# Reordering the step table of an SSD layer: conv product, z weight, skip product, output scale and weight slices

## The chip, the cores and the metric

The kernel runs on one core of one Trainium2 chip. The metric is device time in microseconds (us), from the start to the end of one execution; three executions are timed and the median stands. The engines are TensorE (PE in the profile, with its weight loads as PEld), VectorE (DVE), ScalarE (ACT), GpSimd (POOL) and SyncE (SP), which here issues nearly all transfers.

## The reference

The reference is one inference step of a two-layer decoder over 1024 prompt rows and 8 x 8 sample rows of width 1024, in float32: a Mamba-2 SSD layer, then a latent attention (MLA) layer, then a norm. Only the SSD layer is touched.

```
proj = h @ w_in                           # -> z (2048), x | B | C (2048 + 1024 + 1024), dt (32 heads)
xbc  = silu(causal_conv(xbc, w[0..3]) + b)
dt   = softplus(dt_raw + dt_bias);  a = cumsum(dt * a_head)       # per head, in chunks of 128 rows
M    = exp(a_l - a_s) * (l >= s)
y    = (C B^T * M) (x dt) + (C . state) * exp(a)                  # state runs from chunk to chunk
y    = (y + d_skip * x) * silu(z)
y    = y * rsqrt(mean over a group of 256 (y^2) + eps) * norm_w   # 8 groups
out  = y @ w_out                                                  # 2048 -> 1024
```

B and C are shared by the four heads (256 columns) of a group; there are 8 groups. The outputs are the layer's rows, the final state for the prompt and for each sample, and the last three rows before the convolution.

## The kernel before, in words

Float32 matmuls are done as three products of two-part numbers: a `split` makes a high part (an ACT cast, `L130`, e.g. `wih` from the raw weight `wraw`) and a low part (a subtraction on DVE or POOL, `L131`, e.g. `wil`), and PE multiplies high by high, low by high and high by low.

The layer goes through the 8 groups in a pipeline. While group g-1 is scanned (`Scan`), group g is projected and convolved (`Flow`). `ssd_groups` is one table of steps, written out by hand: from here on the order in which an engine gets its instructions is exactly the order of the calls (the part ahead of it in `layer_ssd` is ordered by a planner). Seven iterations have 21 steps each (t = 0 to 20). A step calls, in this order: `fl.proj(t)` (projection on PE; t = 0 to 11 are the four conv blocks B, C, x, x of 128 channels in three column pieces, t = 12 to 20 are z for nine row tiles), the next weight part's split and load, `scan.ew(t)` (elementwise work of the scan), `fl.ew(t)` (elementwise work of the convolution), `ev()` (ACT copies the projection from PSUM into `raw` or `z`), `fl.after(t)`, `scan.pe(t)` and `fl.pe(t)` (matmuls of the scan, transposes).

In `Scan`, chunk i (0 to 7 for the prompt, 8 for the samples) has its even step t = 2i and its odd step t = 2i+1. The odd step calls `front1(i+1)`: the decay matrix M, for which the cumulative sums are loaded from memory (`M<-acs_d`), ACT relus (`L717`), the Exp (`L723`), the casts of C (`Ch`) and of the weighted x (`xddh`). The `skip` product `xD = x * d_skip` is on POOL (`L731`), `out2` adds it (`L779`), multiplies by the gate (`L786`) and squares with a sum (`L787`) into `yssq`. The samples' states come three at a time: `copies` (`xr`, POOL `L795`), transposes `x3p`, block products `sn`, and the split of the old state `s0p` into `sh` and `sl` for the product `pv`. `split(11)` is the last part of z's weight; it comes at t = 11 behind all of `scan.ew`.

The convolution of a block in `fl.ew` is an ACT product with the fourth tap (`L617`, `acc<-raw`), then three DVE multiply-adds (`L621`) in steps t = 3(b+1) to 3(b+1)+2 for block b, over 128 x 1112 elements.

Behind the groups stands the output stage, a loop of 45 steps. The last group is scanned in its first 22. The product with `w_out` goes in two halves: `OutProj` a over slices 0 to 7 (groups 0 to 3) from step A0 = 7, and b over slices 8 to 15 from step B0 = 25, each over nine row tiles, two steps a tile. A tile of y is loaded back from memory (`yta`, `ytb`), scaled by the reciprocal root of its group's mean square (`scale`, one POOL multiplication, `L998`), transposed on PE (`ytpa`, `ytpb`, `L1008`), split, and multiplied (`poa`, `pob`). `WOut` loads slices of 512 KB (`wraw`) and splits them with the norm weight folded in (`woh` on ACT, `L1062`; `wol` on DVE, `L1068`). `group_rstd` computes the reciprocal roots with a POOL power (`L1087`).

At the start, `layer_ssd` projects group 0, then `ssd_dt` computes dt and the cumulative sums and stores them to memory, and `ssd_groups` begins with the first chunk's `load_decay`, `front`, `front1`, and then loads and splits group 1's first weight parts.

## Time and profile before

| what | value |
|---|---|
| three runs | 2110.97, 2112.72, 2114.36 us; median 2112.72 |
| profiled execution | 2108.55 us, its span 2106.5 us, granted clock 0.963 |
| PE busy | 1935.1 us (92% of the span) |
| DVE, ACT, POOL busy | 1251.3, 1078.6, 840.4 us |
| start of group 1 to the end of group 7 | about 126 to 863 us, 101.5 us for a middle group |
| output stage with the last scan | about 863 to 1032 us |
| output product alone | about 1032 to 1140 us, then the MLA layer |

The profile comes from one execution. A row of the timeline has the start, the duration, the engine, the line, the operation, the tile written and the tiles read with their shapes, and in brackets how long the engine was idle before it and what ended that wait. A row of the busy time by stretch has the stretch, its length, then for PE, PEld, DVE, ACT and POOL the busy time and the count, then the granted TensorE clock as a share of the full one, the share of the DMA engines that was busy, and GB/s. A row of the costliest groups has line, engine, operation, tiles and count, then busy time and mean ns, then the idle time before them.

### The profile page before, as it was taken

To read this page: it belongs to the slowest core of one execution; us is meant where nothing else is said; L and a number is where in the kernel's file an instruction comes from. 1 tells how busy PE (TensorE), PEld (TensorE's weight loads), DVE (VectorE), ACT (ScalarE), POOL (GpSimd) and SP (SyncE) were. 2 spreads that over 40 slices of the span, in tenths; PEclk is the share of its full clock that TensorE was granted. 3 is DMA by queue.
4 is the path that set the end of the run, shared out by engine and by line. 5 is a ranking of instruction groups with operands and counts; after the bars stand their busy time and mean duration, and the time that the engine had idled before them with its cause. 6 is when DMAs were issued, how large, how long until landed. Compare 5 with 4: busy or idle time off the path is not lost.

```text
span 2106.5 us, 33533 instructions
## 1 busy us (share of the span) xinstructions
PE 1935.1 (92%) x12001; PEld 1765.0 (84%) x12001; DVE 1251.3 (59%) x2540; ACT 1078.6 (51%) x2555; POOL 840.4 (40%) x1003
## 2 busy tenths in 40 slices
PE   6969999999999999589999999799999999889998
PEld 5969999999999998578787999698888788778887
DVE  4427575858585757534424305366787878776665
ACT  5345656565656565622203314244676667755552
POOL 0316464737474757433210001102333333765541
PEclk9979999999999999689999999899999999999999
DMA  4013232332323232533645333132111211464441
GB/s 144 20 54 88 82 86 82 90 88 80 91 85 92 81 88 75 169 115 131 199 152 183 112 139 86 41 108 78 47 42 43 63 38 54 131 194 137 143 148 43
DMA packets 186477, 206.54 MB, mean 98 GB/s; under 512 B 23132, under 2 KB 151912, under 8 KB 185928
## 3 DMA queue, kind: packets, MB, share of 16 engines
q1 hardware_dynamic: 181480, 185.40, 29.2%
q0 software_dynamic: 4752, 18.88, 2.8%
q8 instruction: 95, 1.56, 0.3%
q14 instruction: 70, 0.57, 0.1%
q10 hardware_dynamic: 80, 0.13, 0.0%
HBM read 151.05 MB, written 53.28 MB: 97 GB/s over the span
## 4 chain that ended last, share of the span: by engine, by line
PE 60%; DVE 15%; ACT 7%; issue 6%; DMA 6%; POOL 5%; SPq 1%; POOLq 0%; DVEq 0%; ACTq 0%
PE pj L89 19%; PE pq L101 5%; PE pob L101 4%; PE poa L101 4%; PE pj L101 3%; PE py L742 2%; POOL kvl L1961 2%; PE pk L101 1%; PE pz L101 1%; PE p L101 1%; DVE tl L1680 1%; PE vp L89 1%; DMA M<-acs_d 1%; PE st L1666 1%; PE st L1668 1%
## 5 line engine op out<-in xcount | busy, mean ns | idle before, releaser
L89 PE MATMUL pj<-xh,wih 128*128 128x384 f32 (+1 forms) x768 | 254.9, 336 | 18.4 <-ACT wih L130 9.8
L89 PE MATMUL pj<-xl,wih 128*128 128x384 f32 (+1 forms) x768 | 254.4, 331 | 0.0
L89 PE MATMUL pj<-xh,wil 128*128 128x384 f32 (+1 forms) x768 | 252.6, 329 | 0.0
L621 DVE SCALAR_TENSOR_TENSOR acc<-raw,vec,acc 128x1112 f32<-128x1112 f32 x84 | 138.0, 1643 | 77.7 <-ACT acc L617 77.7
L89 PEld LDWEIGHTS pj<-xh,wih 128*128 128x128 f32 x768 | 145.4, 190 | 20.1 <-ACT wih L130 10.1
L1680 POOL TENSOR_TENSOR tl<-P,th 128x384 fp32r<-128x384 f32 (+1 forms) x96 | 90.4, 942 | 179.1 <-ACT P L1678 143.5
L101 PE MATMUL pj<-wih,xh 128*128 128x256 f32 x504 | 144.2, 290 | 3.9 <-ACT wih L130 3.9
L89 PEld LDWEIGHTS pj<-xl,wih 128*128 128x128 f32 x768 | 146.2, 190 | 0.6
L89 PEld LDWEIGHTS pj<-xh,wil 128*128 128x128 f32 x768 | 145.8, 190 | 0.2 <-DVE wil L131 0.2
L101 PE MATMUL pj<-wil,xh 128*128 128x256 f32 (+1 forms) x504 | 140.0, 284 | 4.0 <-DVE wil L131 4.0
L1677 ACT ACTIVATE th<-st 128x512 fp32r<-128x512 f32 x192 | 94.1, 490 | 72.2 <-PE st L1673 53.3
L101 PE MATMUL pj<-wih,xl 128*128 128x256 f32 x448 | 126.7, 283 | 0.0
L131 DVE TENSOR_TENSOR wil<-wraw,wih 128x512 fp32r<-128x512 f32 x88 | 70.3, 802 | 92.0 <-ACT wih L130 91.6
L131 POOL TENSOR_TENSOR xddl<-xdd,xddh 128x256 fp32r<-128x256 f32 x64 | 65.5, 1024 | 127.5 <-ACT xddh L130 126.5
L779 POOL TENSOR_TENSOR y<-y,xD 128x256 f32<-128x256 f32 x64 | 77.9, 1217 | 78.0 <-DVE y L778 78.0
L1961 POOL TENSOR_TENSOR kvl<-pgr,kvh 128x1024 fp32r<-128x1024 f32 x32 | 78.2, 2444 | 65.6 <-ACT kvh L1960 65.6
L101 PEld LDWEIGHTS pj<-wih,xh 128*128 128x128 f32 x504 | 96.2, 191 | 5.3 <-ACT wih L130 5.3
L101 PEld LDWEIGHTS pj<-wil,xh 128*128 128x128 f32 (+1 forms) x504 | 93.2, 185 | 6.0 <-DVE wil L131 5.4
L717 ACT ACTIVATE M<-M,tok 128x128 f32<-128x128 f32 (+1 forms) x288 | 90.5, 388 | 11.5 <-DMA M<-acs_d 11.5
L1678 ACT ACTIVATE P<-st 128x512 f32<-128x512 f32 x192 | 93.2, 486 | 0.0
L130 ACT CAST Ch<-acc 128x128 fp32r<-128x128 f32 x56 | 16.9, 301 | 137.3 <-PE py L89 137.1
L101 PEld LDWEIGHTS pj<-wih,xl 128*128 128x128 f32 x448 | 85.7, 191 | 0.0
(999 smaller groups left out, 6457.1 us busy)
## 6 DMA issues: line engine op xcount, KB each, us to landing
wraw<-in_ssd_w_in SPq DMA_DIRECT2D x92, 256.0 KB
M<-acs_d SPq DMA_DIRECT2D x64, 256.0 KB
y_d<-xD SPq DMA_DIRECT2D x64, 128.0 KB
s<-in_state_ssm SPq DMA_DIRECT2D x32, 256.0 KB
out_s_ssm<-s SPq DMA_DIRECT2D x32, 256.0 KB
wraw<-in_ssd_w_out SPq DMA_DIRECT2D x16, 512.0 KB
q_d<-qt SPq DMA_DIRECT2D x32, 192.0 KB
qp<-q_d SPq DMA_DIRECT2D x8, 768.0 KB
```

Of the source, the lines that this page charges most:

```text
L89: nc.tensor.matmul(out, a, b, start=(i == 0), stop=(i == n - 1))
L101: nc.tensor.matmul(o, a, b, start=(j == 0), stop=(j == len(ops) - 1))
L131: (eng or nc.vector).tensor_tensor(lo, src, hi.bitcast(F32), op=ALU.subtract)
L621: nc.vector.scalar_tensor_tensor(acc, raw[:, j : j + n], k.convw[j][:, blk : blk + 1], acc, op0=ALU.mult, op1=ALU.add)
L717: nc.scalar.activation(M[:m, h, :m], M[:m, h, :m], AF.Relu, bias=c.tk[:, 0, 4 * g + h : 4 * g + h + 1], scale=-1.0)
L742: nc.tensor.matmul(py[:m, h * 64 : h * 64 + 64], c.M[:m, h, :m], c.xdt[:m, h * 64 : h * 64 + 64], start=True, stop=True)
L779: nc.gpsimd.tensor_tensor(y[:m], y[:m], c.xD[:m], op=ALU.add)
L1666: nc.tensor.matmul(ps[:, :n], kh[:, ks], qh[:, qs], start=True, stop=False)
L1677: nc.scalar.activation(th[:, :n], ps[:, :n], AF.Exp, scale=SCALE)
L1678: nc.scalar.activation(P[:, :n], ps[:, :n], AF.Exp, scale=SCALE)
L1680: eng.tensor_tensor(tl[:, :n], P[:, :n], th[:, :n].bitcast(F32), op=ALU.subtract)
L1961: nc.gpsimd.tensor_tensor(rl, raw, rh.bitcast(F32), op=ALU.subtract)
```

## The change

In the group table: the ACT product of the convolution is emitted in `after(t)` of steps 2, 5, 8, 11, right behind the evacuation that completes its `raw`, by the new `conv0`. The three multiply-adds of the last block move from t = 12, 13, 14 to t = 14, 15, 16. `skip` moves from step 2i to step 2i+1. The second `copies` moves from t = 12 to t = 11. The split of weight part 11 moves into `front1`, between the split of C and the relus.

In the output stage: `scale` is four ACT copies with a scale, one for each group of 256 columns. `group_rstd` works tile by tile, in place. `w_out` has three raw buffers in the place of four, two slices are split in each of steps 0 to 3, slices 8 and 9 in steps 5 and 6; slices 10 and 11 are loaded at step 7 into a second pool and split at step 21; the last four are split at step 22. The first tile of y for b is loaded at step 21. A0 is 5 and B0 is 23, so the loop has 43 steps.

At the start: group 1's first four loads and two splits are called ahead of `ssd_dt`, in the part that the planner orders, and the object is handed to `ssd_groups`.

```diff
@@ -602,23 +602,19 @@
         k, g, nc = self.k, self.g, self.k.nc
         bi, j = divmod(t, 3)
         bi -= 1
-        if 0 <= bi < 4:
-            blk = (16 + g, 24 + g, 2 * g, 2 * g + 1)[bi]
-            raw, n = self.raw[bi], RAW - 3
-            if bi % 2 == 0 and j == 0:
-                acc = self.ap.tile([128, 2, n], F32, tag=f"acc{bi // 2}", name=f"acc{g}{bi // 2}", bufs=1)
-                xs = self.ap.tile([128, 2, NB * NT], F32, tag=f"xs{bi // 2}", name=f"xs{g}{bi // 2}", bufs=1)
-                self.xc.append((acc, xs))
-            acc = self.xc[bi // 2][0][:, bi % 2]
+        if 0 <= bi < 4 and j == 0:
+            raw = self.raw[bi]
+            smp = raw[:, 3 + SEQ :].rearrange("p (b w) -> p b w", w=NT + 3)
             if t == 3:
                 self.ct = self.gp.tile([128, 4, 27], F32, tag="ct", name=f"ct{g}")
-            if j == 0:
-                smp = raw[:, 3 + SEQ :].rearrange("p (b w) -> p b w", w=NT + 3)
-                nc.scalar.activation(acc, raw[:, 3:], AF.Identity, bias=k.convb[:, blk : blk + 1],
-                                     scale=k.convw[3][:, blk : blk + 1])
-                nc.gpsimd.tensor_copy(self.ct[:, bi, 0:3], raw[:, SEQ : SEQ + 3])
-                nc.gpsimd.tensor_copy(self.ct[:, bi, 3:].rearrange("p (b w) -> p b w", w=3), smp[:, :, NT:])
-            nc.vector.scalar_tensor_tensor(acc, raw[:, j : j + n], k.convw[j][:, blk : blk + 1], acc,
+            nc.gpsimd.tensor_copy(self.ct[:, bi, 0:3], raw[:, SEQ : SEQ + 3])
+            nc.gpsimd.tensor_copy(self.ct[:, bi, 3:].rearrange("p (b w) -> p b w", w=3), smp[:, :, NT:])
+        if t > 11:
+            bi, j = 3, t - 14
+        if 0 <= bi < 4 and 0 <= j < 3:
+            blk, n = self.blk(bi), RAW - 3
+            acc = self.xc[bi // 2][0][:, bi % 2]
+            nc.vector.scalar_tensor_tensor(acc, self.raw[bi][:, j : j + n], k.convw[j][:, blk : blk + 1], acc,
                                            op0=ALU.mult, op1=ALU.add)
         if t < 12 and t % 3 == 1:
             bi = t // 3
@@ -641,7 +637,26 @@
             for o, n, c in ((0, 128, DIN + 128 * g), (128, 128, DIN + 1024 + 128 * g), (256, 256, 256 * g)):
                 nc.sync.dma_start(k.O["p_conv"][0, 0, :, c : c + n], self.co[0:3, o : o + n])
                 nc.sync.dma_start(sc[:, c : c + n], self.co[3:27, o : o + n])
+    def last_part(self):
+        self.split(11)
+
+    def conv0(self, bi):
+        k, g, nc = self.k, self.g, self.k.nc
+        blk, n = self.blk(bi), RAW - 3
+        if bi % 2 == 0:
+            acc = self.ap.tile([128, 2, n], F32, tag=f"acc{bi // 2}", name=f"acc{g}{bi // 2}", bufs=1)
+            xs = self.ap.tile([128, 2, NB * NT], F32, tag=f"xs{bi // 2}", name=f"xs{g}{bi // 2}", bufs=1)
+            self.xc.append((acc, xs))
+        nc.scalar.activation(self.xc[bi // 2][0][:, bi % 2], self.raw[bi][:, 3:], AF.Identity,
+                             bias=k.convb[:, blk : blk + 1], scale=k.convw[3][:, blk : blk + 1])
+
+    def blk(self, bi):
+        g = self.g
+        return (16 + g, 24 + g, 2 * g, 2 * g + 1)[bi]
+
     def after(self, t):
+        if t < 12 and t % 3 == 2:
+            self.conv0(t // 3)
         if t == 20:
             z = self.z[2]
             self.k.nc.scalar.activation(z[:, :2], z[:, :2], AF.Silu)
@@ -692,7 +707,7 @@
         pc = c.cb = self.bank("cb", "cb" + c.tag)
         nc.tensor.matmul(pc[:m, :m], c.B, c.C, start=True, stop=True)
 
-    def front1(self, i):
+    def front1(self, i, mid=None):
         k, nc, g, hs = self.k, self.k.nc, self.g, self.hs
         c = self.c[i]
         m, tag, p, M = c.m, c.tag, c.trp, c.M
@@ -713,6 +728,8 @@
         if 0 < i < 8:
             c.Ch, c.Cl = (self.tile([128, 128], "C" + x, "C" + x + tag, 1, F32R) for x in "hl")
             split(k, c.Ch, c.Cl, c.C, nc.gpsimd)
+        if mid:
+            mid()
         for h in range(4):
             nc.scalar.activation(M[:m, h, :m], M[:m, h, :m], AF.Relu, bias=c.tk[:, 0, 4 * g + h : 4 * g + h + 1], scale=-1.0)
 
@@ -868,7 +885,7 @@
     def add_state(self, n):
         self.k.nc.vector.tensor_tensor(self.s0[n], self.s0[n], self.sn.rearrange("p (b n) -> p b n", b=4), op=ALU.add)
 
-    def ew(self, t):
+    def ew(self, t, mid=None):
         k, nc = self.k, self.k.nc
         i, odd = divmod(t, 2)
         if t == 12:
@@ -896,8 +913,6 @@
                 self.state(i - 1)
                 c = self.c[i - 1]
                 self.out1(c, c.py, c.py[:, 256:] if i > 1 else None)
-            if i <= 8:
-                self.skip(i)
         else:
             if t in (15, 17, 19, 21):
                 self.add_state((t - 15) // 2)
@@ -905,11 +920,13 @@
                 self.split_state((t - 13) // 2)
             if i < 8:
                 self.fade(i)
-                self.front1(i + 1)
+                self.front1(i + 1, mid)
+            if i <= 8:
+                self.skip(i)
             if 1 <= i <= 8:
                 self.out2(self.c[i - 1])
-        if t in (9, 12):
-            self.copies(t == 12)
+        if t in (9, 11):
+            self.copies(t == 11)
         if t == 11:
             self.third(0)
         if t in (12, 17):
@@ -980,7 +997,7 @@
         self.nk = 8
         self.y, self.xr, self.p, self.yhl = {}, {}, {}, {}
         self.ng = self.nk // 2
-        self.rs = k.rs
+        self.rs = k.yssq[:, :, k0 // 2 : k0 // 2 + self.ng]
 
     def load_y(self, i):
         k, (t0, m) = self.k, TILES[i]
@@ -995,7 +1012,8 @@
 
     def scale(self, i):
         y, m = self.y[i], TILES[i][1]
-        self.k.nc.gpsimd.tensor_tensor(y[:m], y[:m], self.rs[:m, i].unsqueeze(2).to_broadcast([m, self.ng, 256]), op=ALU.mult)
+        for g in range(self.ng):
+            self.k.nc.scalar.activation(y[:m, g], y[:m, g], AF.Copy, scale=self.rs[:m, i, g : g + 1])
 
     def turn(self, i):
         nc, m = self.k.nc, TILES[i][1]
@@ -1074,32 +1092,22 @@
     return (yb, ya) * 4 + (yb,)
 
 
-A0, B0 = 7, 25
-
-
-def group_rstd(k, g0, part=None):
-    nc = k.nc
-    if not part:
-        k.rs = k.cs.tile([128, 9, 4], F32, tag="yrs", name=f"yrs{g0}", bufs=1)
-        nc.vector.tensor_scalar(k.rs, k.yssq[:, :, g0 : g0 + 4], 1.0 / 256, EPS, op0=ALU.mult, op1=ALU.add)
-    r = k.rs if part is None else k.rs[:, part]
-    e = k.nhalf[:, : 36 if part is None else 4]
-    nc.gpsimd.tensor_tensor(r, r, e if part is not None else e.rearrange("p (a b) -> p a b", a=9), op=ALU.pow)
-
-
-def ssd_groups(k, g0, pools, sp, psum, st, left, right, als):
+A0, B0 = 5, 23
+
+
+def group_rstd(k, g0, i):
+    r = k.yssq[:, i, g0 : g0 + 4]
+    k.nc.vector.tensor_scalar(r, r, 1.0 / 256, EPS, op0=ALU.mult, op1=ALU.add)
+    k.nc.gpsimd.tensor_tensor(r, r, k.nhalf[:, :4], op=ALU.pow)
+
+
+def ssd_groups(k, g0, nxt, pools, sp, psum, st, left, right, als):
     tc, nc = k.tc, k.nc
     pscan = None
     scan = Scan(k, g0, (sp, psum))
     scan.load_decay(0)
     scan.front(0)
     scan.front1(0)
-    nxt = Flow(k, 1, pools)
-    for p in range(2):
-        nxt.load(p)
-    for p in range(2):
-        nxt.split(p)
-        nxt.load(p + 2)
     for g in range(1, G):
         fl, nxt = nxt, Flow(k, g + 1, pools) if g < G - 1 else None
         nscan = Scan(k, fl, (sp, psum))
@@ -1114,25 +1122,23 @@
             if nxt and t == 18:
                 nxt.split(0)
                 nxt.load(2)
-            scan.ew(t)
+            scan.ew(t, fl.last_part if t == 11 else None)
             if t == 0 and pscan:
                 pscan.ew(21)
             if t == 17:
                 nscan.load_decay(0)
             if t == 20:
                 nscan.front1(0)
-            if t == 11:
-                fl.split(11)
-                if nxt:
-                    nxt.load(1)
+            if t == 11 and nxt:
+                nxt.load(1)
             fl.ew(t)
             if t < 9 and not nxt:
                 group_rstd(k, 0, t)
             if t == 18 and not nxt:
                 als.close()
                 wrs = ExitStack()
-                wo = WOut(k, wrs.enter_context(open_pool(tc, name="wor", bufs=1, side="right")), 4)
-                for kk in range(4):
+                wo = WOut(k, wrs.enter_context(open_pool(tc, name="wor", bufs=1, side="right")), 3)
+                for kk in range(3):
                     wo.load(kk)
             ev()
             fl.after(t)
@@ -1158,17 +1164,21 @@
             scan.ew(t)
         if t == 0:
             pscan.ew(21)
-        if t < 5:
-            for kk in ((0, 1), (2, 3), (4,), (5, 6), (7,))[t]:
+        if t < 4:
+            for kk in (2 * t, 2 * t + 1):
                 wsa.append(wo.split(kk, wa))
-        if t == 5:
-            wsb.append(wo.split(8, wx))
-        if t < 6:
+        if t in (5, 6):
+            wsb.append(wo.split(t + 3, wx))
+        if t < 7:
             wo.low()
-            for kk in ((4, 5), (6, 7), (8,), (), (), ())[t]:
+            for kk in ((3, 4), (5, 6), (7, 8), (9,), (), (), ())[t]:
                 wo.load(kk)
+        if t == 7:
+            wrs.close()
+            wo = WOut(k, st.enter_context(open_pool(tc, name="wor2", bufs=1)), 2)
+            wo.load(10)
+            wo.load(11)
         if t == 21:
-            wrs.close()
             right.close()
             h0 = k.h0.enter_context(open_pool(tc, name="h0", bufs=1, side="right"))
             k.h0p = h0
@@ -1176,17 +1186,21 @@
             k.sqp = lambda name: k.tok.rearrange("p i a h -> p (i a h)")[:, :D]
             yb = st.enter_context(open_pool(tc, name="yb", bufs=1, side="right"))
             wb = st.enter_context(open_pool(tc, name="wob", bufs=1, side="right"))
-            wo = WOut(k, st.enter_context(open_pool(tc, name="wor2", bufs=1, side="right")), 2)
-            wo.load(9)
-            wo.load(10)
+            for kk in (10, 11):
+                wsb.append(wo.split(kk, wb))
+                wo.low()
+                wo.load(kk + 2)
+            ob = OutProj(k, YORD(yb, ya), wsb, psum, NWA, h_loader(k), "b")
+            ob.load_y(0)
+        if 4 <= t <= 18 and t % 2 == 0:
+            group_rstd(k, 4, t // 2 - 2)
         if t == 22:
-            group_rstd(k, 4)
-            ob = OutProj(k, YORD(yb, ya), wsb, psum, NWA, h_loader(k), "b")
+            group_rstd(k, 4, 8)
         for o, T in ((oa, A0), (ob, B0)):
             if o:
                 o.ew(t - T)
-        if 21 <= t < 25:
-            for kk in ((9,), (10, 11), (12, 13), (14, 15))[t - 21]:
+        if t == 22:
+            for kk in (12, 13, 14, 15):
                 wsb.append(wo.split(kk, wb))
                 wo.low()
                 if kk < 14:
@@ -1251,13 +1265,19 @@
             load_zdt(k, p0)
             for _ in st0:
                 pass
+            f1 = Flow(k, 1, pools)
+            for p in range(2):
+                f1.load(p)
+            for p in range(2):
+                f1.split(p)
+                f1.load(p + 2)
             ssd_dt(k, p0, psum)
         sp = right.enter_context(open_pool(tc, name="sp", bufs=2, side="right"))
         k.cblk = [sp.tile([128, 4, 64], F32R, name=f"cblk{q}") for q in range(2)]
         for t in k.cblk:
             nc.gpsimd.memset(t.bitcast(F32), 0.0)
         with tc.manual_schedule(engines={e.engine for e in (nc.tensor, nc.vector, nc.scalar, nc.gpsimd, nc.sync)}):
-            ssd_groups(k, g0, pools, sp, psum, st, left, right, als)
+            ssd_groups(k, g0, f1, pools, sp, psum, st, left, right, als)
     stc.close()
 
 
```

## The prediction

> **What bounds the kernel now.** I read the page first (busy shares, chain, costliest groups), then the busy time by stretch, then PE's timeline wherever the chain left PE, and at each such place the timelines of the engines that PE waited for.
>
> ```profile
> PE 1935.1 (92%) x12001; PEld 1765.0 (84%) x12001; DVE 1251.3 (59%) x2540; ACT 1078.6 (51%) x2555; POOL 840.4 (40%) x1003
> PE 60%; DVE 15%; ACT 7%; issue 6%; DMA 6%; POOL 5%; SPq 1%; POOLq 0%; DVEq 0%; ACTq 0%
> L621 DVE SCALAR_TENSOR_TENSOR acc<-raw,vec,acc 128x1112 f32<-128x1112 f32 x84 | 138.0, 1643 | 77.7 <-ACT acc L617 77.7
> ```
> PE is busy 92% of the span, so the edits, none of which takes a matmul away, can at most remove PE's idle time. The last row is the convolution's chain on VectorE: it idles 77.7 us waiting for ScalarE's first product.
>
> ```profile
> 126.00:242.00 116.00, 102.42 (x734) 99.39 (x733) 66.63 (x113) 61.35 (x164) 56.64 (x81) 0.93 0.29 82
> 445.50:547.00 101.50, 98.15 (x724) 96.08 (x722) 67.47 (x114) 62.19 (x166) 57.71 (x82) 1.00 0.30 87
> 863.00:960.00 97.00, 69.81 (x333) 59.69 (x334) 43.19 (x78) 33.94 (x94) 43.21 (x55) 0.78 0.37 120
> 1032.00:1140.00 108.00, 106.78 (x499) 85.97 (x497) 34.52 (x50) 16.32 (x28) 16.46 (x12) 1.00 0.48 154
> ```
> The columns are the stretch and its length, then busy time of PE, PEld, DVE, ACT and POOL, granted clock, DMA share and rate. Rows: the first group with the start, a middle group, the output stage under the last scan, the pure output projection. In a middle group PE has 101.50 - 98.15 = 3.35 us idle. The start has 13.58 us, and the output stage 27.19 us at a clock of 0.78. The last stretch has 1.22 us: there PE alone sets the pace, and edits on other engines cost nothing.
>
> **The change, part by part.**
>
> *Weights ahead of dt.* What holds PE at the start:
>
> ```profile
> 138.58 0.69 PE L89 MATMUL pj<-xh,wih 128*128 128x384 f32 x1 [9.85 <-ACT wih L130]
> 136.74 1.28 ACT L717 ACTIVATE M<-M,tok 128x128 f32<-128x128 f32 x4 [7.87 <-DMA M<-acs_d]
> 137.92 1.12 ACT L130 CAST wih<-wraw 128x512 fp32r<-128x512 f32 x2
> 132.50 0.58 SPq L674 DMA_DIRECT2D M<-acs_d  x1
> 133.17 10.86 SPq L543 DMA_DIRECT2D wraw<-in_ssd_w_in  x5
> 142.81 0.63 ACT L723 ACTIVATE M<-M 128x512 f32<-128x512 f32 x1
> 149.34 1.00 PE L742 MATMUL py<-xdt,M 128*128 128x64 f32 x8
> 59.06 11.25 DVE L469 SCALAR_TENSOR_TENSOR acc<-raw,vec,acc 128x1112 f32<-128x1112 f32 x6 [3.26 <-ACT acc L466]
> 69.67 0.49 PE L89 MATMUL pj<-xh,wih 128*128 128x320 f32 x1 [3.38 <-ACT raw L453]
> ```
> Group 1's weight casts stand on ScalarE behind the decay's relu, which waits for the transfer of M, and their loads on SyncE behind that transfer. Moved ahead, the four loads, two casts (1.12 us) and two subtractions lie before 128, and the projection can start where the wait begins, at 138.58 - 9.85 = 128.73. The next limit is the first back step (149.34), which needs M: landed at 136.7, relu 1.28, then Exp 0.63, cast and split; without the weight casts and the two load waits between, I work it out to about 140.5. So 149.3 - 140.5 = 8.8 us comes off (no more than the 9.85 of the wait; the projection matmuls fill the time before). The price: the two subtractions go into VectorE's chain at 59.06, which PE's wait at 69.67 ends on: at most 2 x 0.69, of which I take 0.7. If the loads on SyncE delay the decay's inputs as well, the gain falls to 6. Net -8 (-9 to -6).
>
> *Conv product sooner, skip in odd steps, copies a step earlier, z weight inside the front (7 groups).* PE's waits of the middle group, and what ended them:
>
> ```profile
> 508.49 0.39 PE L101 MATMUL pj<-wih,xh 128*128 128x256 f32 x1 [0.37 <-ACT wih L130]
> 509.45 0.39 PE L101 MATMUL pj<-wil,xh 128*128 128x256 f32 x1 [0.58 <-DVE wil L131]
> 516.65 0.72 PE L801 MATMUL x3p3True<-ident,xr3True 128*96 128x128 f32 x3 [0.89 <-POOL xr3True L795]
> 522.01 0.63 PE L839 MATMUL s0p<-ident,s 128*128 128x128 f32 x4 [0.76 <-issue]
> 523.20 0.50 PE L865 MATMUL sn<-bb3False,x33False 96*128 96x512 f32 x1 [0.56 <-DVE S L765]
> 506.09 1.28 ACT L717 ACTIVATE M<-M,tok 128x128 f32<-128x128 f32 x4
> 507.27 0.40 ACT L787 ACTIVATE y<-xD 128x256 f32<-128x256 f32 x1
> 507.82 0.62 ACT L130 CAST wih<-wraw 128x512 fp32r<-128x512 f32 x1
> 513.18 1.31 ACT L617 ACTIVATE acc<-raw,vec 128x1112 f32<-128x1112 f32 x1
> 514.63 1.75 POOL L731 TENSOR_TENSOR xD<-xsT,dsk 128x256 f32<-128x256 f32 x1
> 518.53 2.73 DVE L621 SCALAR_TENSOR_TENSOR acc<-raw,vec,acc 128x1112 f32<-128x1112 f32 x1
> ```
> The five waits are 3.16 us, nearly all of the 3.35. Counted as start-to-start distance over the usual pitch of the same matmul they cost 0.53 + 0.84 + 1.05 + 0.88 + 0.75 = 4.05. Each has one cause that the change takes away:
> - The z weight's cast (507.82) stands behind four relus (1.28) and the square (0.40); inside the front it comes over 1.3 us sooner, and so does its subtraction: 1.37 goes. The relus and the Exp come 0.62 later; what they feed is a step away, and ScalarE is busy 62.19 of 101.50.
> - xr3True's copies stand on GpSimd behind the skip product (1.75): a step sooner, 1.05 goes. GpSimd's queue then has the 0.67 of copies ahead of the odd step's products, and the skip product after them; the y square that reads it is at the step's end.
> - The matmuls at 522.01 and 523.20 wait for small VectorE work behind the 2.73 us multiply-add, which ends at 518.53 + 2.73 = 521.26 (the profile names no releaser for the first; two short VectorE operations lie between). Its last block moves from steps 12 to 14 to steps 14 to 16: 0.88 + 0.75 goes at that place, but two more multiply-adds stand ahead of the last steps' chain to the gate and the state product. There I expect the wait now shown as "<-DVE sl" to grow by about 0.55, and x3p to keep 0.3.
> - The ScalarE product (1.31) moves from behind the elementwise work of the step to right behind the evacuation it reads: VectorE's 77.7 us of idle time shrinks. It costs nothing while ScalarE has slack; without that cover it costs 1.31 in four steps a group.
>
> 4.05 - 0.85 = 3.2 a group. Bounds: 1.5 (two of the waits come back elsewhere) and 4.1. Seven groups: -22.4 (-29 to -10).
>
> *Output stage: w_out, scale, per-tile rstd, A0 and B0.*
>
> ```profile
> 901.44 1.10 PE L1008 MATMUL ytpa<-ident,yta 128*128 128x128 f32 x8 [2.65 <-POOL yta L998]
> 902.29 0.48 PE L101 MATMUL poa<-woh,yha 128*128 128x512 f32 x1
> 909.91 0.48 PE L101 MATMUL poa<-woh,yha 128*128 128x512 f32 x1
> 915.26 0.40 PE L101 MATMUL poa<-woh,yla 128*128 128x512 f32 x1
> 1019.80 0.58 SPq L988 DMA_DIRECT2D ytb<-y_d  x1
> 1026.18 1.90 POOL L998 TENSOR_TENSOR ytb<-ytb,yrs 128x1024 f32<-128x1024 f32 x1 [0.44 <-DMA ytb<-y_d]
> 1019.59 6.14 POOL L1087 TENSOR_TENSOR yrs<-yrs,nhalf 128x36 f32<-128x36 f32 x1 [10.17 <-DVE yrs L1084]
> 1028.13 1.17 PE L1008 MATMUL ytpb<-ident,ytb 128*128 128x128 f32 x8 [4.10 <-POOL ytb L998]
> 857.71 2.18 ACT L1062 ACTIVATE woh<-wraw,vec 128x1024 fp32r<-128x1024 f32 x2
> 860.19 5.54 SPq L1057 DMA_DIRECT2D wraw<-in_ssd_w_out  x4
> 1016.34 1.15 ACT L1062 ACTIVATE woh<-wraw,vec 128x1024 fp32r<-128x1024 f32 x1 [5.80 <-DMA wraw<-in_ssd_w_out]
> 1041.07 0.48 PE L101 MATMUL pob<-woh,yhb 128*128 128x512 f32 x1
> 1053.06 0.47 PE L101 MATMUL pob<-woh,yhb 128*128 128x512 f32 x1
> ```
> Scale: GpSimd's 1.9 us becomes four ScalarE activations over 256 columns. The nearest row of that size is the square at 507.27, 0.40 each; they queue behind a cast and four relus (1.28), and the transposes start when the first quarter is done. I take 2.1 us of wait for the 2.65, five pairs: -2.5; bounds, none and -7. A0 from 7 to 5: A's first product comes some 7.8 us sooner (an estimate, the scan steps replayed by hand with their changed order), but the steps that then carry a product still wait for VectorE's scan work, so little of this reaches the end. Three raw buffers for four: slice 3 is loaded only after the first casts (issue row at 860.19, wait for its landing about 5 us, by the 5.80), which delays steps 1 to 4 by 1.5 to 4 us. With one more pair of steps that carries both, the last scan step then ends some 10 us later, and fewer of A's products are left behind it.
>
> B's start: the 36-element power (6.14) becomes nine of four elements, of which only one stands there (about 1.0): its wait of 4.10 goes. But the last six slices, 12 casts and subtractions, and y's load are all issued in steps 21 and 22, behind each other, and less of A is left to cover them. y lands some 6 us after its load (1019.80 to the scale at 1026.18); I get 8.8 us of idle PE, and B's second product at 1045.6 to 1047.5 against 1041.07. Output stage in all: +5.5 (-2 to +12); -2 if A's earlier start is kept in full, +12 if PE also waits for slices 14 and 15.
>
> Behind it a pair takes 1053.06 - 1041.07 = 11.99 us of pure PE time, and the four ScalarE scales lie beside it: 0.
>
> Sum: -8 - 22.4 + 5.5 = -25. The profiled run took 2108.55 us (4.2 less than the median of 2112.72): it would become 2083.5, the median 2088.
>
> The clock after an idle stretch: after the 2.65 wait the starts of 24 products and the next pass from 902.29 to 909.91, 7.6 us; the 24 from 909.91 are through at 915.66, 5.7 us. The 8.8 us idle at B's start thus costs up to 2 us of slow clock, which is inside the +5.5. The Trainium skill ("TensorE: Matmul & The Clock Gate", Part 1) has the clock fall to half after an idle window of about 3.4 us and return after as long a busy one. The trace shows a slow start already after 2.65 us of wait: by that rule alone the five waits would not slow the clock.
>
> **Rivals.**
> - *VectorE becomes the bound at the group's end.* The multiply-adds moved to steps 15 and 16 (2.73 in the row, 1.64 in the page's mean) delay the gate and the state product: 2 us a group come back, 1.2 remain. For it: VectorE is the engine with the longest chain there (DVE 15% of the chain). Against: VectorE is busy 67.47 of 101.50. -8 - 8.4 + 5.5 = -11: 2102.
> - *The start gains nothing*, because the transfer of M also holds the first back step. For it: M lands at 136.7 whatever the weights do. -17: 2096.
> - *The clock stays up in A.* If a wait a little shorter keeps the clock from falling, five pairs gain the 7.6 - 5.7 = 1.9 us, about -10 more: 2078. The rule of the Trainium skill named above would have it so for waits under its window. Against it: 2.65 us already slows.
> - *Slower: the conv product on ScalarE.* It stands in steps 2, 5, 8 and 11 ahead of the next step's casts, relus and Exp, which PE waits for in the back step. If all of 1.31 reaches PE, 28 times, it is +36.7, and the sum +12: 2124. It decides from 25 / 28 = 0.9 us a time. Against it: ScalarE idles 39.31 us in a group, and waits on PE for the Ch cast.
>
> **How the numbers follow.** The forecast's own case has 0.50, 2078 to 2100; VectorE at the end 0.20; the start 0.10; the clock 0.08; the ScalarE product, with other losses of that size, 0.12. 2088 is the likeliest. The range goes to 2106 for the VectorE case with a loss of 12 in the output stage, and to 2076 for the best: it leaves out the slower case and some of each end. 0.2% (4.2 us) is about what tells a change from none: faster 0.83, same 0.05 (the worst of the VectorE case), slower 0.12.
>
> **What would show it.** Start: no wait of 9.85 at 138, PE's first py product near 140.5. Groups: 101.5 becomes about 98.3, and the waits at xr3True, wih and s0p are gone; a longer one "<-DVE sl" near step 19 speaks for the first rival, "<-ACT" waits at the py or st products for the last. Output: rows of scale on ACT of about 0.4 x4, ytpa waits near 2.1, the last scan step near ten us later in that stage, one PE gap of 6 to 10 at B's start. I am wrong if the casts in steps 1 to 4 wait much longer for their slices, or if the group's time stays at 101.

## The result, and the profile after

The changed kernel took 2121.40 us in the median of 18 runs (2111.79 to 2128.61), the kernel before 2111.97 in 18 runs: a ratio of 1.0042, with a 95% interval of 1.0024 to 1.0060. It was a little slower where a gain of 25 us was forecast. In a later comparison (e10 below) the same two kernels gave 0.9998 (0.9982 to 1.0014). So the change is worth nothing or costs some 0.4%; that the 25 us didn't come is beyond doubt. The two intervals don't meet, so up to 9 us between two such comparisons can be chance. The profiled execution has a span of 2119.7 us, before 2106.5.

The page of the changed kernel, the row of PE and that of the convolution's multiply-adds (`L621` before, `L617` now):

```profile
PE 1947.4 (92%) x12001; PEld 1776.3 (84%) x12001; DVE 1239.8 (58%) x2556; ACT 1110.2 (52%) x2627; POOL 799.8 (38%) x993
L617 DVE SCALAR_TENSOR_TENSOR acc<-raw,vec,acc 128x1112 f32<-128x1112 f32 x84 | 148.7, 1770 | 0.2
```

VectorE's wait for ScalarE's product is gone (77.7 us before, 0.2 now), as the change meant. But the same 84 multiply-adds now take 148.7 us for 138.0, and PE has the same work and 12 us more busy time.

Where the time is, by landmarks that both traces have (times in us from the start; the last product of the output stage is its last `pob`):

| landmark | before | changed | difference |
|---|---|---|---|
| first projection product of group 1 | 138.58 | 131.46 | -7.12 |
| of group 4 | 445.40 | 438.81 | -6.59 |
| of group 7 | 750.02 | 743.64 | -6.38 |
| first product of the output stage | 890.59 | 878.42 | -12.17 |
| its last product | 1137.64 | 1139.37 | +1.73 |
| span | 2106.5 | 2119.7 | +13.2 |

The start gave what was forecast. The six groups up to group 7 gave nothing (+0.7), where 22.4 us was forecast for seven. From group 7 to the end of the output stage 8.1 us were lost, where 5.5 was forecast for the output stage; e4 below takes the two apart. The rest, 11.5 us, lies in the MLA layer, which the change doesn't touch.

Two neighbouring groups of the changed kernel by stretch (length, busy time of PE, PEld, DVE, ACT, POOL, granted clock, DMA share, GB/s), then the waits of PE in the first of them:

```profile
438.81:539.41 100.60, 97.64 (x723) 95.97 (x721) 65.61 (x114) 62.71 (x166) 56.81 (x82) 1.00 0.31 88
539.41:643.05 103.64, 100.76 (x723) 99.12 (x721) 65.60 (x114) 62.70 (x166) 57.21 (x82) 0.97 0.30 85
```

```profile
503.40 0.63 PE L856 MATMUL s0p<-ident,s 128*128 128x128 f32 x4 [0.63 <-DVE b L829]
518.40 0.36 PE L89 MATMUL st<-xddh,BTh 128*128 128x256 f32 x1 [1.82 <-DVE s L886]
536.27 0.31 PE L877 MATMUL pv<-sl,cblk 128*32 128x128 f32 x2 [0.45 <-DVE sl L131]
```

The five waits of before (wih, wil, xr3True, s0p of step 14, sn) are gone, as forecast. In their place stand three: 0.63 at the s0p product of step 12, which did not wait before, 0.45 for 0.20 at sl, and a new one of 1.82 us at the state product (st) of step 15.

And groups with the same work differ by up to 3 us: of five, two take 100.6 us at a clock of 1.00, two 102.0 to 102.1 at 0.98, and one 103.64 at 0.97. In that last one the clock is at half behind the wait (the wait, then a stretch of 4 us; the granted clock is the third number from the right):

```profile
619.06 0.35 PE L89 MATMUL st<-xddh,BTh 128*128 128x256 f32 x1 [1.80 <-DVE s L886]
622.00:626.00 4.00, 4.00 (x25) 4.00 (x23) 2.30 (x4) 0.00 (x0) 1.70 (x1) 0.50 0.39 111
```

Before, with several waits of 1 us and less, all middle groups ran at 1.00.

What VectorE and GpSimd did ahead of that wait in the first of the two groups; the first row is another multiply-add of the group, with nothing on GpSimd beside it:

```profile
503.18 1.38 DVE L617 SCALAR_TENSOR_TENSOR acc<-raw,vec,acc 128x1112 f32<-128x1112 f32 x1
513.33 0.42 DVE L795 TENSOR_TENSOR y<-y,py 128x256 f32<-128x256 f32 x1
513.67 3.99 DVE L617 SCALAR_TENSOR_TENSOR acc<-raw,vec,acc 128x1112 f32<-128x1112 f32 x1
517.58 0.68 DVE L886 TENSOR_TENSOR s<-s,sn 128x512 f32<-128x512 f32 x1
```

```profile
512.78 0.61 POOL L748 TENSOR_TENSOR xD<-xsT,dsk 128x256 f32<-128x256 f32 x1
513.36 0.73 POOL L131 TENSOR_TENSOR xddl<-xdd,xddh 128x256 fp32r<-128x256 f32 x1
514.05 0.73 POOL L131 TENSOR_TENSOR Sl<-S,Sh 128x256 fp32r<-128x256 f32 x1
514.75 0.73 POOL L796 TENSOR_TENSOR y<-y,xD 128x256 f32<-128x256 f32 x1
515.45 1.03 POOL L864 TENSOR_TENSOR s<-s,decs 128x512 f32<-128x512 f32 x1
516.45 1.69 POOL L776 TENSOR_TENSOR S<-S,decp 128x256 f32<-128x256 f32 x1
```

The multiply-add that the change put into step 14 takes 3.99 us; alone it takes 1.38. GpSimd runs four operations in a row at their usual 0.73 and 1.03 while it lasts; only the fifth (`S<-S,decp`, 1.69 for 0.62) is held up, and the multiply-add ends 1.2 us into that one. By these rows VectorE was held off until GpSimd's train let it in. Everything behind it on VectorE, the small operations that PE waits for, is 2.3 us later than behind a multiply-add of 1.72, which is what this one takes in e13 below. Ahead of the train stands the skip product of step 13 (512.78), which the change moved there.

### The profile page after: what moved, and what is told of

It is laid out like the page before. It is cut to its first block, busy times and chain, and to the rows that moved or that the text cites. A ratio compares the mean times of both kernels' runs of the same rounds, so it can differ in the third digit from the quotient of the medians.

```text
span 2119.7 us, 33702 instructions
## 1 busy us (share of the span) xinstructions
PE 1947.4 (92%) x12001; PEld 1776.3 (84%) x12001; DVE 1239.8 (58%) x2556; ACT 1110.2 (52%) x2627; POOL 799.8 (38%) x993
## 4 chain that ended last, share of the span: by engine, by line
PE 63%; DVE 12%; ACT 8%; issue 7%; DMA 5%; POOL 4%; SPq 1%; POOLq 0%; DVEq 0%; ACTq 0%
PE pj L89 22%; PE pq L101 5%; PE poa L101 4%; PE pob L101 4%; PE py L759 2%; PE pj L101 2%; POOL kvl L1981 2%; PE pz L101 1%; PE pk L101 1%; ACT acc L626 1%; PE p L101 1%; PE vp L89 1%; DVE tl L1700 1%; PE kp L89 1%; PE st L89 1%
## 5 line engine op out<-in xcount | busy, mean ns | idle before, releaser
L617 DVE SCALAR_TENSOR_TENSOR acc<-raw,vec,acc 128x1112 f32<-128x1112 f32 x84 | 148.7, 1770 | 0.2
L796 POOL TENSOR_TENSOR y<-y,xD 128x256 f32<-128x256 f32 x64 | 83.7, 1308 | 92.2 <-DVE y L795 86.2
L131 POOL TENSOR_TENSOR xddl<-xdd,xddh 128x256 fp32r<-128x256 f32 x64 | 60.7, 948 | 134.6 <-ACT xddh L130 134.6
```

Source lines behind the costliest of these rows:

```text
L131: (eng or nc.vector).tensor_tensor(lo, src, hi.bitcast(F32), op=ALU.subtract)
L617: nc.vector.scalar_tensor_tensor(acc, self.raw[bi][:, j : j + n], k.convw[j][:, blk : blk + 1], acc, op0=ALU.mult, op1=ALU.add)
L796: nc.gpsimd.tensor_tensor(y[:m], y[:m], c.xD[:m], op=ALU.add)
```

## The experiments

All ratios are to the kernel before on the same chip; where two runs are compared below, they may come from two chips. In all but e9, e10 and e12 the instruction order of the MLA layer's sample part is held as before, by edits that add no work. In the code, "..." stands for lines left out, and the comments are added here.

**e5: the start alone.** The edit takes everything back but the call order at the start.

```diff
+            f1 = Flow(k, 1, pools)
+            for p in range(2):
+                f1.load(p)
+            for p in range(2):
+                f1.split(p)
+                f1.load(p + 2)
             ssd_dt(k, p0, psum)
```

> The kernel before with only the weights of group 1 ahead of dt. By the profiles (first projection product of group 1 at 131.46 for 138.58) it should be 7 us faster, ratio 0.9967, about 7 us under before. If the start's gain is taken back by a later wait, it shows as less than 3 us.

Ratio 0.9968 (0.9946 to 0.9990), 6.8 us; in the trace the first projection product of group 1 is at 129.78 (-8.8), group 7 at -7.5. The start's gain is real and stays.

**e6: the skip product alone.** The kernel before with the skip product in the odd steps, and nothing else but the held order of the MLA layer.

```diff
-            if i <= 8:
-                self.skip(i)          # even step, behind out1
...
                 self.front1(i + 1)
+            if i <= 8:
+                self.skip(i)          # odd step
```

> The kernel before with only the skip product moved to the odd steps. If the move alone crowds GpSimd beside VectorE's multiply-adds, a group gets 1 to 2 us longer: 7 to 14 us slower than before, ratio 1.003 to 1.007, with the multiply-adds of steps 12 to 14 longer than 1.38, 2.73 and 1.72. If it does harm only together with the multiply-adds in steps 14 to 16, or helps as the step table meant (the xr3True wait of 0.89 gone), it is 0 to 6 us faster, ratio 0.997 to 1.000.

Ratio 1.0159 (1.0124 to 1.0194): 34 us slower, more than twice what was expected. The groups take 106 us and more for 101.5. The trace of this kernel, VectorE and PE, then GpSimd:

```profile
537.27 4.72 DVE L618 SCALAR_TENSOR_TENSOR acc<-raw,vec,acc 128x1112 f32<-128x1112 f32 x1
542.73 0.36 PE L89 MATMUL st<-xddh,BTh 128*128 128x256 f32 x1 [2.75 <-DVE s L885]
```

```profile
537.24 0.73 POOL L131 TENSOR_TENSOR Sl<-S,Sh 128x256 fp32r<-128x256 f32 x1
537.94 0.73 POOL L795 TENSOR_TENSOR y<-y,xD 128x256 f32<-128x256 f32 x1
538.63 1.03 POOL L863 TENSOR_TENSOR s<-s,decs 128x512 f32<-128x512 f32 x1
539.63 0.61 POOL L775 TENSOR_TENSOR S<-S,decp 128x256 f32<-128x256 f32 x1
540.21 0.60 POOL L747 TENSOR_TENSOR xD<-xsT,dsk 128x256 f32<-128x256 f32 x1
```

Five operations in a row, none held up; they end at 540.81, and the multiply-add ends at 541.99, 1.2 us later. It is the multiply-add of step 14 (here the last of the block) that is 4.72 us long for 1.72 before; the other eleven of the group add up to 18.1 us in both kernels. PE then waits 2.75 at the same st product.

**e1 and e2: the change with the skip product back in the even steps.** e1 is the change with the MLA order held, e2 the same with

```diff
+            if i <= 8:
+                self.skip(i)          # even step again
...
-            if i <= 8:
-                self.skip(i)
```

> The changed kernel, with the instruction order of the untouched MLA layer held as in the kernel before: in its sample part the planner had put two weight subtractions (w5l) on VectorE and one weight cast (w5h) on ScalarE ahead of the softmax's small operations, and here they are held behind them. Theory (the planner's new order costs 6 to 7 us, the SSD layer itself +1.7): 6 to 7 us less than the changed kernel, a ratio to before of 1.001, about 2114. Rival (the MLA layer's extra time in the profile is chance, from the clock): no difference to the changed kernel, ratio 1.0042, about 2121.

> As e1, with the skip product back in the even steps. Theory (the multiply-add of step 14, 3.99 us, is slowed by the GpSimd operations beside it, of which the moved skip product is one): it falls to 2.7 or less, PE's wait of 1.82 us at the st product to under 0.6, a group from 102 to 99.5 or less and no clock below 1.00 in the groups; 8 to 14 us less than e1, ratio about 0.996. Rival (the place of the multiply-adds alone makes the wait): it stays at 1.8, and the xr3True wait of 0.9 may come back, time as e1 or up to 5 us more.

e1: 1.0016 (0.9999 to 1.0033). e2: 0.9923 (0.9894 to 0.9953), 16 us faster than before and 20 below e1, more than the 8 to 14 expected. The groups of e2 take 99.3 us at a clock of 1.00, the st wait is gone, and the longest of the groups' 84 multiply-adds is 1.80. The rival, that the place of the multiply-adds alone makes the wait, falls. Of e1 more below.

**e3: the multiply-adds back in steps 12 to 14, the skip product as changed.**

```diff
-            bi, j = 3, t - 14
+            bi, j = 3, t - 12
```

> As e1, with the last block's three multiply-adds back in steps 12, 13 and 14, and all else as changed. Theory (the wait at step 14 comes from the multiply-add placed there beside busy GpSimd, whichever of the three it is): one multiply-add still stands in step 14, so the wait at the st product stays above 1 us and the s0p and sn waits (0.88 and 0.75) come back in part: time within 5 us of e1. Rival (two more multiply-adds late in the group are the cost): the 1.82 wait goes, sl's 0.45 goes, groups fall by 1.5 to 2 each, 10 to 14 us less than e1.

Ratio 0.9976 (0.9956 to 0.9995). The 1.82 wait goes, and the multiply-adds take 1.75, 1.72 and 1.72, which speaks for the rival, but sl keeps its 0.45 and the groups stay at 101.6: a wait of 1.59 at xr3True takes its place. The multiply-add of step 14, GpSimd's operation at its start, and that wait:

```profile
516.57 1.72 DVE L617 SCALAR_TENSOR_TENSOR acc<-raw,vec,acc 128x1112 f32<-128x1112 f32 x1
516.38 0.74 POOL L131 TENSOR_TENSOR Sl<-S,Sh 128x256 fp32r<-128x256 f32 x1 [0.38 <-ACT Sh L130]
509.89 0.53 PE L818 MATMUL x3p3True<-ident,xr3True 128*96 128x128 f32 x3 [1.59 <-DVE sl L131]
```

So the skip product of step 13 alone does not make the wait of 1.82: here it stands where the change put it, but GpSimd idles 0.38 us ahead of Sl, and the multiply-add gets in. With the changed places of all else, it takes the multiply-adds in steps 14 to 16 as well. By the traces the SSD layer ends as in e1 (1137.99 and 1137.71). So the theory was wrong on where the wait would be; that time only moved was right. The 8 us by which e3 ran under e1 lie behind this layer, where the two kernels are the same.

**e13: only the skip product of step 13 back.** The sharpest question: one product of nine.

```diff
+            if i == 6:
+                self.skip(i)          # even step 12
...
-            if i <= 8:
+            if i <= 8 and i != 6:
                 self.skip(i)
```

> As e1 (all of the change), but of the nine skip products of a group only the one of step 13 goes back to its even step 12; the other eight stay in the odd steps. Theory (the loss is one multiply-add, that of step 14, caught behind the GpSimd train that the skip product of step 13 lengthens): the multiply-add falls from 3.99 to 2.3 or less, the wait of 1.82 to under 0.6, and most of e2's gain comes back: 12 to 18 us below e1, ratio 0.993 to 0.996. Rival (each skip product in an odd step holds up the queue a little): 2 to 5 us below e1.

Ratio 0.9894 (0.9866 to 0.9922), 22 us faster than before, above all that was expected. A middle group by stretch, then VectorE's and GpSimd's rows at step 14:

```profile
427.19:525.20 98.01, 97.28 (x722) 95.89 (x721) 63.69 (x114) 62.76 (x166) 58.34 (x82) 1.00 0.31 90
```

```profile
502.61 1.72 DVE L617 SCALAR_TENSOR_TENSOR acc<-raw,vec,acc 128x1112 f32<-128x1112 f32 x1
```

```profile
502.42 0.73 POOL L131 TENSOR_TENSOR Sl<-S,Sh 128x256 fp32r<-128x256 f32 x1
503.12 1.81 POOL L796 TENSOR_TENSOR y<-y,xD 128x256 f32<-128x256 f32 x1
```

The group has 0.73 us of idle PE. The multiply-add now gets in behind Sl, and it is `y<-y,xD` that waits (1.81 for 0.73). The other skip products in odd steps do no harm; they even leave the groups 1.3 us shorter than in e2 (98.0 and 99.3).

**e14: the multiply-adds back in steps 12 to 14, the skip product even.** e2 with e3's edit.

> As e2 (skip product in the even steps), with the last block's multiply-adds back in steps 12 to 14. If moving them was worth its place once the skip product stays: the s0p and sn waits of 0.88 and 0.75 come back, 1 to 1.6 us a group, 7 to 11 us above e2, ratio about 0.997. If the earlier conv product is enough (the multiply-adds then stand where GpSimd is quiet): as e2 within 3 us, ratio 0.992.

Ratio 0.9948 (0.9923 to 0.9972), by the trace 11.7 us above e2 at the end of the layer (5 by the ratios, with overlapping intervals); the waits at s0p and sn are back (0.41 and 0.56), and one of 1.59 at xr3True. By the traces, moving the multiply-adds was worth its place.

**e4, e7, e8 and e15: the output stage.** e4 is e1, e7 is e2 and e15 is e13, each with the output stage of before (A0 = 7, B0 = 25, four raw buffers, scale and roots as before). e8 is e7 with the roots tile by tile:

```diff
-            group_rstd(k, 4)                       # step 22, 36 elements
+        if 4 <= t <= 18 and t % 2 == 0:
+            group_rstd(k, 4, t // 2 - 2)           # 4 elements each
...
+            group_rstd(k, 4, 8)                    # step 22
```

> The start and the group table as changed, the output stage (scale on GpSimd, weight slices, per-tile roots, the two start steps 7 and 25) as before, MLA order as before. By the two profiles the start gives -7.1, the groups +0.7 and the output stage +8.1: I expect -6.4 against before, ratio 0.997, about 2105.5. If the output stage's loss came from what the group table hands over (the last group's late chain), it stays at +1.7 or more.

> As e2 (all of the change but the skip product, which stays in the even steps), with the output stage of before. In e2 the groups end 22.5 us ahead of before and the output stage gives 3.8 back. If the changed output stage is the loss: 20 to 23 us faster than before, ratio 0.990. If the output stage's loss comes with the earlier parts (its first steps start late either way), it stays at e2's 16 to 18, ratio 0.992.

> As e7, with the reciprocal roots taken tile by tile (the only part of the changed output stage kept). The 36-element power (6.14 us) goes from the start of the second half and with it PE's wait of 4.10: 4 us faster than e7, ratio about 0.988. If the load of y is what the second half waits for anyway, no more than 0.5 us.

> As e13, with the output stage of before. In e13 the groups end 28.7 us ahead of before and the output stage gives 3.8 back by the end of the layer. If its loss is the changed output stage's own (e7 against e2: 7.7 us in the traces), this is 30 to 33 us faster than before, ratio 0.985; if not, as e13, 0.989.

e4: 0.9981 (0.9959 to 1.0002), e7: 0.9875 (0.9845 to 0.9905), e8: 0.9877 (0.9846 to 0.9908), e15: 0.9838 (0.9814 to 0.9862). The old output stage is better in each pair (e4 against e1, e7 against e2, e15 against e13), though two pairs' intervals overlap and the third pair's are 0.0004 apart. e15 has the best median of all, 34 us faster than before. Its profile doesn't show the gain (the layer ends at 1111.73, in e13 at 1112.75, in e7 at 1111.26), and its profiled run, 2094.05 us, is above its median of 2080.49: one profile says little about 10 us.

e4 came out between what was expected and the rival: the layer ends 2.5 us ahead of before, not 6.4. From the start of group 7 to the end of the layer e1 loses 8.25 us against before, and e4, with the old output stage, still 4.25. So only about half of that loss is the changed output stage's; the rest comes with the last group. By the same measure e2 and e7 differ by 9.6, e13 and e15 by 2.7.

What costs in the changed output stage, in the changed kernel's trace:

```profile
909.72 1.97 PE L1026 MATMUL ytpa<-ident,yta 128*128 128x128 f32 x8 [2.25 <-ACT yta L1016]
1029.15 1.97 PE L1026 MATMUL ytpb<-ident,ytb 128*128 128x128 f32 x8 [10.16 <-ACT ytb L1016]
1028.59 1.71 ACT L1016 ACTIVATE ytb<-ytb,yssq 128x256 f32<-128x256 f32 x4 [9.27 <-DMA ytb<-y_d]
1019.62 1.55 SPq L1075 DMA_DIRECT2D wraw<-in_ssd_w_out  x2
1021.22 0.42 SPq L1005 DMA_DIRECT2D ytb<-y_d  x1
```

The four scales on ScalarE take 1.71 together, and the wait of this pair is 2.25 for 2.65. At the second half's start PE waits 10.16 us: the load of y is issued at 1021.22, behind two weight loads on SyncE, and the scale starts 7.4 us later. In e8 the 36-element power is gone and PE still waits 3.37 (e7: 3.43), for the load; the tile-by-tile roots alone bring nothing.

**e9 to e12: the MLA layer.** The planner had given VectorE and ScalarE another order in the MLA layer's sample part: a weight subtraction (w5l) ahead of the softmax's maximum and scale, a weight cast (w5h) ahead of its exponential. e9 and e10 are the kernel before and the changed kernel once more, e11 is e1 once more, and e12 puts the new order into the kernel before.

> The kernel before once more, for a second profile: ratio 1.000. If the length of the untouched MLA layer (829.9 us from the first cached-key transpose to the last product in the profile of before) is a property of the program, it comes back within 2 us; if it is chance of the granted clock from run to run, it differs by 5 us or more.

> The changed kernel once more: ratio 1.0042 within its interval. Its MLA layer took 842.3 us in the same measure: within 2 us again if it is the program's, and the stretch in which w5l stands ahead of the softmax (48.0 us against 40.7) again near 48.

> e1 once more, beside the changed kernel on the same chip. Theory (the planner's order): 5 to 7 us below e10, and the stretch of w5l near 41 to 45. Rival (chance of the clock): no difference between the two beyond their intervals.

> The kernel before with the changed kernel's order of the MLA layer's sample part put into it: one w5h cast on ScalarE ahead of the softmax's exponential, one w5l subtraction on VectorE ahead of its maximum. Theory (the planner's order costs): 3 to 7 us slower than before, ratio 1.0015 to 1.0035, the stretch at 44 to 48 us. Rival: within 0.001 of before, the stretch at 41.

e9: 1.0002 (0.9983 to 1.0020), e10: 0.9998 (0.9982 to 1.0014), e11: 1.0019 (0.9997 to 1.0040), e12: 1.0006 (0.9991 to 1.0022): no difference between any two. From the first cached-key transpose to the last product the layer took 829.9 and 831.3 us in the two profiles of before, 842.4 and 836.8 in those of the changed kernel, 847.4 and 841.0 in e1 and e11, 838.0 in e12, and 829.5 to 843.1 in the other ten, all with the order held. So e10's second profile did not come back within the 2 us that were expected. The stretch with w5l (first product of sc41n to first of sc42n) took 40.7 twice, 48.0 and 46.7, 45.5 and 45.4, 41.4, and 40.7 to 45.4 in the other ten, named in the same order. So the theory that the planner's order costs 6 to 7 us falls: moved into the kernel before it took 41.4, and held back 40.7 to 45.5. Why that stretch is longest in the changed kernel is open. Most of the rest moves with the granted clock: from the first to the last st product of the attention e14 took 376.5 us at a clock of 0.96, and e1 391.4 at 0.92.

## Why the prediction was wrong

- **The start (-8): right.** Measured -7.1 in the changed kernel's trace, -9.6 in its second (e10), -8.8 in e5's, and -6.8 in e5's runs. The price in VectorE's chain, 0.7, is less sure: the subtraction moved there took 3.13 us (0.69 in its usual place) beside an operation of 3.72 on GpSimd, where a multiply-add had taken 3.77 before, and the matrix product that the chain leads to came at 125.25 for 122.17, but at 122.81 in e10. The rival "The start gains nothing" falls: the first py product came at 143.24 for 149.34.
- **The groups (-22.4): the step that failed is the skip product, to which the prediction gave no price.** It said of GpSimd's queue that the odd steps' products stand behind the copies "and the skip product after them", and looked only at who reads the product. There it was wrong too: the reader is GpSimd's own `y<-y,xD`, in the next even step and in the same train (this addition stands in `out1`, not in `out2`). It didn't look at what a longer train of GpSimd operations does to VectorE, though its own row of before (2.73 for a multiply-add that takes 1.38) showed it. One skip product of nine, that of step 13, cost 25 us (the layer ends at 1137.71 in e1 and at 1112.75 in e13), with the multiply-adds in steps 14 to 16; in steps 12 to 14 all nine cost 7 (1137.99 in e3, 1130.60 in e14). The other working held: with that one taken back a group is 3.43 us shorter than before (six groups from 138.58 to 750.02 and from 130.40 to 721.29), where 3.2 was forecast and 4.05 was the bound.
- **The rival "VectorE becomes the bound at the group's end" named the place, the state product, but only half of the cause.** Its mark, a longer wait for sl, isn't what came: sl grew from 0.20 to 0.45, and the new wait is at the st product. The rival said the later multiply-adds as such would do it, for 2 us a group. e2 and e13 leave them where they are and lose nothing, and e14 shows that they gain; e3 shows that without them the wait at st goes too.
- **The rival "the conv product on ScalarE" didn't come about:** no wait of PE for it in the groups.
- **The rival "The clock stays up in A" came about in places only:** behind the 2.25 us wait at 909.72 the clock was 0.80 for the next 8.3 us, behind an equal one at 927.74 it stayed at 1.00.
- **The output stage (+5.5): right in sign; its size is not settled.** The loss from group 7 on is 8.1, of which e4 against e1 puts about 4 on the output stage's own changes. The wait at the second half's start, 8.8 forecast, is 10.16; the scales' wait, 2.1 forecast, is 2.25 in the row shown; the last scan step came 13 us later against the groups' end (966.10 and 972.76 at the last cb product, from -6.4 to +6.7), where 10 was said.
- **The clock.** The page of the Trainium skill, "TensorE: Matmul & The Clock Gate", Part 1, has a free-running window of some 3.4 us and lets the clock fall after an idle one. Here a wait of 1.8 us was followed by the half clock in some groups (0.97 in the mean, 103.64 us) and not in others (1.00, 100.60 us), with the same rows in both. The trace does not agree that a wait must be that long; that a free-running window meets the wait in some groups only would fit, but no run shows it. The prediction counted no clock loss in the groups; it is 1.4 to 3 us in each that is met.
- **The MLA layer:** taken as unmoved, and within what the runs can tell it is.

The sum of the prediction, -25, is what the change gives without that one move: e13 gives -22 by its runs and -24.9 at the end of the layer in the trace; with the old output stage it is -34 by the runs (e15).

## What to carry to other kernels

When work moves on GpSimd, look at what VectorE has in flight at that moment, not only at who reads the result: a long VectorE operation that begins behind a train of ready GpSimd operations can last until the train ends. A row that is twice as long in one place as elsewhere is the sign of it, and it should be priced before anything is put next to it. And of a step table with several edits, the one that was given no price is the first to be run alone.

## What the runs showed of the hardware that was not expected

- The 128 x 1112 multiply-add takes 1.36 to 1.38 us alone, 1.72 to 1.78 when it gets in after the GpSimd operation that is running, and 3.99 and 4.72 when it doesn't; then it ends about 1.2 us after GpSimd's train gave way. The Trainium skill ("Advanced Engine Details and Errata", GPSIMD Details) has GpSimd share a read and a write interface with VectorE, in conflict with VectorE's instructions that have two inputs in SBUF. The trace agrees (the multiply-add reads raw and acc), and adds that GpSimd can hold VectorE off through five operations of its own (3.6 us). What decides who gets in is open: in e13 the multiply-add began 0.19 us after Sl and got in behind it, in e6 it began 0.03 us after Sl and didn't. One reading fits these rows, and no run tests it: the multiply-add gets in when GpSimd's next operation is still not ready shortly after the running one has begun. Behind Sl that is `y<-y,xD`, and its input from VectorE came 0.27 us after Sl began in e13 and e3, 0.11 after in e6, and 0.30 before Sl in the changed kernel.
- The same program's layer differs by 6 us between two profiles of one kernel (842.4 and 836.8), and one profiled run was 13.6 us above the median of its kernel (e15).
